# PEER grids: a turn after each of the first four one-hot steps of a tile

## The chip, the cores and the metric

The kernel runs on one core of one Trainium2 chip. The metric is the device time of one execution in microseconds, here the median of several executions. One execution was also taken by the hardware profiler; its trace is what the rows below come from.

## What is computed

The reference runs three transformer layers on 512 tokens of width 1024, in float32: a layer with an RWKV-7 time mix and a SwiGLU, a layer with a spatial gating unit and a SwiGLU, and a layer with two kinds of attention and a PEER feed-forward. The change lies in the PEER part alone, which the reference writes so:

```
q = (hb @ w_q).reshape(C, PEER_HEADS, 2, PEER_DK_HALF)
s = einsum('thpd,hpnd->thpn', q, sub_keys)
sv, si = lax.top_k(s, PEER_TOPK)
cand = sv[:, :, 0, :, None] + sv[:, :, 1, None, :]
cidx = si[:, :, 0, :, None] * PEER_NKEYS + si[:, :, 1, None, :]
fv, fpos = lax.top_k(cand, PEER_TOPK)
eidx = take_along_axis(cidx, fpos)          # 8 heads x 16 = 128 experts of 16384 for each token
g = softmax(fv)
a = gelu(einsum('ted,td->te', u_tab[eidx], hb))
return einsum('te,ted->td', g * a, v_tab[eidx])
```

## The kernel before

The tokens are four tiles of 128. The kernel treats tile 0 and tiles 1 to 3 of the PEER part in two different ways.

**Tiles 1 to 3, dense.** The 16384 experts are 128 groups of 128. `act(j)` loads group j of the u table (512 KB, `wload`, queue SP), splits it into a high part `whi` (ScalarE) and a low part `wlo` (VectorE; for every fifth group GpSimd), multiplies both with the 384 tokens in 24 matmuls (L122 to L124, `mm3`) and puts the gelu into `gl` (L1274). The generator `ahead` runs `act` for the first 112 groups ahead of their use and stores each `gl` to DRAM as `ga[j]` (L1279, queue of GpSimd); `fill(n)` takes n of these steps. The last 16 groups are made inside the last loop (`late_act`, tile `gla`). Below, "an act" is one such step.

**The grids.** How much weight a token gives to each expert is built as a 128 x 128 grid for each token: the product of a one-hot matrix of the expert's first index (scaled by the softmax weight in two float16 parts, `oi`) and one of its second index (`oj`). `onehots(t)` makes both for four tokens at a time, one set, in four steps on VectorE: `on` (L1451, copied to `oj` by ScalarE, L1452), `os` (L1454), and `oi` twice (L1457). There are two buffers for `on` and `os` and three for `oi` and `oj`. `grids(t)` first runs four such steps (HL = 4, so one set ahead). Then, 32 times for a tile, it runs four more steps, multiplies the oldest set in eight matmuls (L1477) and copies the bank into `G` (ScalarE, L1479). `G` goes to DRAM in pieces of 512 KB (`spill`, tile `gd`, queue SP), but for the last two of twelve, which stay on chip.

**Tile 0, gathered.** `own` fetches the 128 chosen u rows and then the 128 chosen v rows of tile 0's tokens by indirect DMA (L1297, 512 KB each, up to five ahead) and does one VectorE pass over each (L1309 with an accumulator read for u, L1313 for v): 256 steps. `some(x)` adds x to a debt and takes a step for each whole one.

**How the work is interleaved.** `picks(t)` finds the top experts of a tile on VectorE (L1342 to L1436) and gives a turn back 14 times. At each turn the driver at the end of `peer` lets `unit(prev, 3)` take three turns of the grids of the tile before. Each turn that `grids` gives back also pays for other work: FG = 0.6508 acts (FL = 0.7484 in tile 3) and S2 = 0.7 steps of `own` (SL = 0.8 in tile 3). After the last tile, `fill(NS)` takes the acts that are left, and the last loop over all 128 groups begins: it loads `ga[j]` back into `gl` (L1571, queue SP), multiplies it with the grid table `gte` or `gtl` (L1573, read from `gd` by L1549 in pieces of 640 KB for four groups, queue of GpSimd) and with the `G` on chip (L1575), splits it (`ch`, `cl`), loads a group of the v table and does 18 matmuls. Each round pays for S3 = 1.2492 steps of `own`.

The Python order is not the order on the engines: a scheduler places the instructions on each engine's queue when the program is built, and the engines run these queues in order.

The four lines that the change stands in:

```
hot = onehots(t, hots)
for _ in range(HL):
    next(hot)
for c in range(128 // CT):
```

Of the kernel before, what the change touches and what calls it, by code (L numbers as in the profile page):

```python
# [40 lines left out]
class Kern:  # L41
# [1198 lines left out]
    def peer(self):  # L1240
# [8 lines left out]
        with ExitStack() as cx:  # L1249
# [192 lines left out]
            def onehots(t, done):  # L1442
                sh = [128, OT // 4, 128, 4]
                of = lambda v: v.rearrange("p (g t) -> p g t", t=4)[:, :, None, :].to_broadcast(sh)
                io = io4[:, None].to_broadcast(sh)
                for tk in range(t * 128 - 128, t * 128, OT):
                    os, on = [q4.tile(sh, F16, name=n) for n in ("os", "on")]
                    oi = q4.tile([128, 2] + sh[1:], F16, name="oi", bufs=OB)
                    oj = q4.tile([128, OT, 128], F16, name="oj", bufs=OB)
                    done.append((oi, oj))  # L1450
                    nc.vector.tensor_tensor(on, io, of(JT[:, tk:tk + OT]), op=OP.is_equal)  # L1451
                    nc.scalar.copy(oj, on.rearrange("p g i t -> p (g t) i"))  # L1452
                    yield
                    nc.vector.tensor_tensor(os, io, of(IT[:, tk:tk + OT]), op=OP.is_equal)  # L1454
                    yield
                    for w in range(2):
                        nc.vector.tensor_mul(oi[:, w], os, of(WW[:, w, tk:tk + OT]))  # L1457
                        yield

            def grids(t):  # L1460

                gout = iter(())
                hots = []
                hot = onehots(t, hots)
                for _ in range(HL):
                    next(hot)
                for c in range(128 // CT):
                    G = gp.tile([128, 128, CT], F32, name="G")
                    for u in range(0, CT, 4):
                        bk = self.bank("x")  # L1470
                        for _ in range(16 // OT):
                            next(hot, None)
                        if u % OT == 0:
                            oi, oj = hots.pop(0)
                        for e in range(4):
                            for w in range(2):
                                mm(bk[:, e * 128:(e + 1) * 128], oi[:, w, u % OT // 4, :, e], oj[:, u % OT + e],  # L1477
                                   start=(w == 0), stop=(w == 1))
                        nc.scalar.activation(G[:, :, u:u + 4], bk.rearrange("p (t j) -> p j t", t=4), AF.Copy,  # L1479
                                             scale=1.0 / WSC)  # L1480
                        if u % 8 == 4:
                            next(gout, None)
                        yield
                    n = (t - 1) * (128 // CT) + c
                    gout = spill(n, G)
                    if n >= CD - KG:
                        last.append(G)
                        gout = iter(())
                for _ in gout:
                    pass  # L1490

            def spill(c, G):
                for k in range(0, 128, 2048 // CT // 2):
                    n = 2048 // CT // 2
                    nc.sync.dma_start(gd[c, 0:128, k * CT:(k + n) * CT], G[:, k:k + n].rearrange("p j t -> p (j t)"))
                    yield
# [19 lines left out]
            for t in range(NT):  # L1516
                if t == 0:
                    for _ in picks(t):
                        pace(FA, 0)
                    for u in range(1, NT):  # L1520
                        for _ in tops(u):
                            pace(FT, S0)
                    cs.close()
                    q4 = cy.enter_context(tc.tile_pool(name="pe3b", bufs=2))
                    gp = cx.enter_context(tc.tile_pool(name="pegg", bufs=2, side="right"))
                    prev = iter(())
                    continue
                for _ in picks(t):
                    pace(FB, S1)
                    unit(prev, 3)  # L1530
                unit(prev, 128)
                late[0] = t - 1
                prev = grids(t)
# [155 lines left out]
```

## Time and profile before

| | |
|---|---|
| median of 3 executions | 3034.14 us (3032.5 to 3037.2) |
| the profiled execution | 3031.09 us |
| its span in the trace | 3029.4 us |
| TensorE (PE) busy | 2900.9 us, 96% |
| VectorE (DVE) busy | 2090.2 us, 69% |
| ScalarE (ACT) busy | 1208.0 us, 40% |
| GpSimd (POOL) busy | 641.1 us, 21% |

The profile's shares are averages over the whole span; the PEER part, from about 1710 us on, has several stretches with different limits, so it is read by stretches. In the trace the first one-hot row of tile 1 starts at 1993.6 us, that of tile 2 at 2121.2 us and that of tile 3 at 2243.5 us; the last grid matmul ends at 2354.3 us, the last act of the tail at 2391.9 us. A matmul's end is modelled and overlaps the next one's start, so for TensorE the time of a step is taken from counts and stretches rather than from the mean of one row.

### The profile page before, as it was taken

The numbers are of one execution on the slowest core, as the hardware profiler recorded it, in microseconds if no ns is written. First come the engines' busy times: TensorE is split into PE (matmuls) and PEld (weight loads), VectorE is DVE, ScalarE is ACT, GpSimd is POOL, SyncE is SP. The second block draws the span as 40 slices with busy tenths as digits, with TensorE's granted clock in tenths as the row PEclk, the third lists the DMA queues.
The fourth block names the chain that finished last, engine by engine and source line by source line (L and its number), as shares of the span: only waits on it lengthen the run. The fifth ranks groups of instructions, "written<-read, shape, count | busy, mean of one in ns | idle before, by whom it ended". The sixth has DMA issues, their size and how long they took to land.

```text
span 3029.4 us, 43851 instructions
## 1 busy us (share of the span) xinstructions
PE 2900.9 (96%) x16121; PEld 2438.7 (81%) x16121; DVE 2090.2 (69%) x4710; ACT 1208.0 (40%) x2014; POOL 641.1 (21%) x577
## 2 busy tenths in 40 slices
PE   7988989999999999999999999989999999999998
PEld 6867877888888788888875888888999888878787
DVE  6774776333255766425776678999998478878787
ACT  5544333322223422223565433355655333333332
POOL 1022220000000000000000003335455344444443
PEclk9989999999999999999988999999999999999999
DMA  4357553323333277432220234679889899999896
GB/s 142 98 145 213 142 143 115 102 93 95 93 132 103 79 246 237 135 91 90 84 72 8 70 96 165 226 244 320 292 326 322 298 319 345 327 330 318 304 328 225
DMA packets 218579, 569.05 MB, mean 188 GB/s; under 512 B 64474, under 2 KB 80090, under 8 KB 218236
## 3 DMA queue, kind: packets, MB, share of 16 engines
q1 hardware_dynamic: 144508, 362.71, 36.7%
q0 software_dynamic: 62816, 196.70, 19.0%
q10 hardware_dynamic: 11040, 6.84, 0.8%
q8 instruction: 127, 2.08, 0.3%
q14 instruction: 88, 0.72, 0.1%
HBM read 504.24 MB, written 61.87 MB: 187 GB/s over the span
## 4 chain that ended last, share of the span: by engine, by line
PE 66%; DVE 17%; DMA 9%; issue 4%; ACT 3%; POOL 1%; DVEq 0%; POOLq 0%; ACTq 0%; SPq 0%
PE b L276 20%; PE b L124 12%; PE b L123 12%; PE b L122 12%; DMA gl<-ga 4%; DVE wlo L103 3%; DVE er L1309 2%; DVE oi L1457 1%; DVE hr L1313 1%; PE b L1166 1%; DMA wst<-in_pe_v 1%; PE b L1477 1%; PE b L964 1%; PE b L1184 1%; DVE cl L103 1%
## 5 line engine op out<-in xcount | busy, mean ns | idle before, releaser
L102 ACT CAST whi<-wst 128x1024 fp32r<-128x1024 f32 (+2 forms) x491 | 510.6, 1042 | 1067.2 <-PE b L123 334.6
L103 DVE TENSOR_TENSOR wlo<-wst,whi 128x1024 fp32r<-128x1024 f32 (+2 forms) x466 | 563.4, 1210 | 425.2 <-ACT whi L102 408.5
L124 PE MATMUL b<-hTh,wlo 128*128 128x384 f32 (+2 forms) x1992 | 716.5, 360 | 15.1 <-DVE wlo L103 14.9
L122 PE MATMUL b<-hTh,whi 128*128 128x384 f32 (+2 forms) x1992 | 722.5, 363 | 2.5 <-ACT hTh L223 1.5
L123 PE MATMUL b<-hTl,whi 128*128 128x384 f32 (+2 forms) x1992 | 717.2, 360 | 2.2 <-DVE hTl L224 2.2
L124 PEld LDWEIGHTS b<-hTh,wlo 128*128 128x128 f32 x1992 | 378.5, 190 | 58.6 <-DVE wlo L103 21.1
L122 PEld LDWEIGHTS b<-hTh,whi 128*128 128x128 f32 x1992 | 379.0, 191 | 42.0 <-ACT hTh L223 2.2
L123 PEld LDWEIGHTS b<-hTl,whi 128*128 128x128 f32 x1992 | 379.1, 190 | 40.8 <-DVE hTl L224 3.0
L123 PE MATMUL b<-wlo,ch 128*128 128x512 f32 x768 | 306.6, 399 | 6.2 <-DVE wlo L103 6.1
L122 PE MATMUL b<-whi,ch 128*128 128x512 f32 x768 | 306.3, 399 | 5.2 <-ACT ch L102 5.2
L124 PE MATMUL b<-whi,cl 128*128 128x512 f32 x768 | 306.3, 399 | 1.3 <-DVE cl L103 1.3
L1297 POOL DMA_INDIRECT er<-in_pe_v,ev x128 | 196.0, 1531 | 248.0 <-DVE hr L1313 222.3
L1297 POOL DMA_INDIRECT er<-in_pe_ur,eu x128 | 174.0, 1360 | 88.6 <-DVE er L1309 57.7
L123 PEld LDWEIGHTS b<-wlo,ch 128*128 128x128 f32 x768 | 145.8, 190 | 42.2 <-DVE wlo L103 8.0
L122 PEld LDWEIGHTS b<-whi,ch 128*128 128x128 f32 x768 | 145.8, 190 | 39.9 <-ACT ch L102 5.5
L124 PEld LDWEIGHTS b<-whi,cl 128*128 128x128 f32 x768 | 145.8, 190 | 36.7 <-DVE cl L103 2.0
L1309 DVE SCALAR_TENSOR_TENSOR er<-er,hr 128x1024 f32<-128x1024 f32 x128 | 161.9, 1269 | 10.1 <-DMA er<-in_pe_ur,eu 10.1
L1313 DVE SCALAR_TENSOR_TENSOR hr<-er,a,hr 128x1024 f32<-128x1024 f32 x127 | 166.8, 1313 | 0.1
L1279 POOL DMA_DIRECT2D ga<-gl x112 | 64.9, 579 | 318.7 <-ACT gl L1274 307.5
L276 PE MATMUL b<-whi,hTh 128*128 128x512 f32 (+2 forms) x336 | 129.4, 387 | 0.8 <-ACT P L976 0.8
L276 PE MATMUL b<-whi,hTl 128*128 128x512 f32 (+2 forms) x336 | 129.5, 386 | 0.4 <-DVE hTl L103 0.4
L276 PE MATMUL b<-wlo,hTh 128*128 128x512 f32 (+2 forms) x336 | 129.7, 386 | 0.0
(557 smaller groups left out, 4911.8 us busy)
## 6 DMA issues: line engine op xcount, KB each, us to landing
wst<-in_pe_u SPq DMA_DIRECT2D x128, 512.0 KB, 5.4
wst<-in_pe_v SPq DMA_DIRECT2D x128, 512.0 KB, 6.1
wst<-in_ffn_gu SPq DMA_DIRECT2D x88, 512.0 KB, 3.3
wst<-in_ad_w SPq DMA_DIRECT2D x48, 512.0 KB, 3.9
wst<-in_ffn_dn SPq DMA_DIRECT2D x44, 512.0 KB, 3.6
ga<-gl POOLq DMA_DIRECT2D x112, 192.0 KB, 4.9
gl<-ga SPq DMA_DIRECT2D x112, 192.0 KB, 5.3
gd<-G SPq DMA_DIRECT2D x40, 512.0 KB, 8.1
```

Of the source, the lines that this page charges most:

```text
L102: self.nc.scalar.copy(hi, src)
L103: (eng or self.nc.vector).tensor_sub(lo, src, hi)
L122: mm(out, a[0], b[0], start=start, stop=False)
L123: mm(out, a[0], b[1], start=False, stop=False)
L124: mm(out, a[1], b[0], start=False, stop=stop)
L276: self.nc.tensor.matmul(banks[t][:, :n], self.chunk(aT, a, k + kk)[:, t * 128:(t + 1) * 128], w[b][:, kk, :], start=seen[t] == 1, stop=see ...
L964: self.nc.tensor.transpose(bk[:, c * 128:(c + 1) * 128], src[:, c * 128:(c + 1) * 128], self.ident)
L1166: mm(ob[:, h * 128:(h + 1) * 128], PT[:, k, :], v[k][:, h, :], start=(k == 0), stop=(k == t))
L1279: nc.gpsimd.dma_start(ga[j], act(j))
L1297: d = nc.gpsimd.indirect_dma_start(out=r, out_offset=None, in_=src, in_offset=bass.IndirectOffsetOnAxis(ap=idx[:, k:k + 1], axis=0))
L1309: d = nc.vector.scalar_tensor_tensor(r, r, 1.0, hr, op0=OP.mult, op1=OP.mult, accum_out=a0[:, k:k + 1])
L1313: d = nc.vector.scalar_tensor_tensor(y0, r, a0[:, k - 128:k - 127], y0, op0=OP.mult, op1=OP.add)
```

## The change

`grids` now gives a turn back after each of the first four one-hot steps of a tile:

```diff
@@ -1464,6 +1464,7 @@
                 hot = onehots(t, hots)
                 for _ in range(HL):
                     next(hot)
+                    yield
                 for c in range(128 // CT):
```

So a tile's grids give 36 turns instead of 32, and the driver pays for acts and steps of `own` at 108 turns instead of 96. No constant is changed: 72 turns at 0.6508 and 36 at 0.7484 make 73.8 acts where it were 65.6, and 72 at 0.7 and 36 at 0.8 make 79.2 steps of `own` where it were 70.4. With the 39 acts that other places take, all 112 are taken before `fill(NS)`, where eight were left for it. No instruction is added or removed on any engine; they stand in another order. Lines behind the change carry a number that is higher by one.

**VectorE, the beginning of tile 1's grids** (`wlo` belongs to an act, `er` to a step of `own`; `on`, `os` and two `oi` are one set of four tokens). Before:

```order
L103 TENSOR_TENSOR wlo<-wst,whi 128x1024
L1451 TENSOR_TENSOR on<-io_14630,JT 128x512
L1454 TENSOR_TENSOR os<-io_14630,IT 128x512
L1451 TENSOR_TENSOR on<-io_14630,JT 128x512
L1457 TENSOR_TENSOR oi<-os,WW 128x512 x2
L1454 TENSOR_TENSOR os<-io_14630,IT 128x512
L1451 TENSOR_TENSOR on<-io_14630,JT 128x512
L1457 TENSOR_TENSOR oi<-os,WW 128x512 x2
L1309 SCALAR_TENSOR_TENSOR er,a_14638<-er,hr 128x1024
```

Now:

```order
L103 TENSOR_TENSOR wlo<-wst,whi 128x1024
L1451 TENSOR_TENSOR on<-io_14630,JT 128x512
L1309 SCALAR_TENSOR_TENSOR er,a_14638<-er,hr 128x1024
L1454 TENSOR_TENSOR os<-io_14630,IT 128x512
L1309 SCALAR_TENSOR_TENSOR er,a_14638<-er,hr 128x1024
L1457 TENSOR_TENSOR oi<-os,WW 128x512
L1309 SCALAR_TENSOR_TENSOR er,a_14638<-er,hr 128x1024
L1457 TENSOR_TENSOR oi<-os,WW 128x512
L1451 TENSOR_TENSOR on<-io_14630,JT 128x512
L1454 TENSOR_TENSOR os<-io_14630,IT 128x512
L103 TENSOR_TENSOR wlo<-wst,whi 128x1024
L1457 TENSOR_TENSOR oi<-os,WW 128x512 x2
```

Steps of `own` and a split stand between the first set's four steps. On TensorE three acts, 72 matmuls, now stand ahead of the first grid matmul of each tile; before, the first grid matmuls of tiles 1 and 2 stood inside an act.

**GpSimd's queue at the end of tile 3's grids** (`ga` is the store of an act, and its number counts up to 14616 for the last one; `gte` and `gtl` are the grid tables of the last loop). Before:

```order
L1279 DMA ga_14605<-gl 128x384
L1549 DMA gte<-gd 128x10x128 x2
L103 TENSOR_TENSOR wlo<-wst,whi 128x1024
L1279 DMA ga_14606<-gl 128x384
L1297 DMA er<-in_pe_ur,eu 128x1024
L1549 DMA gtl<-gd 128x10x128
L1279 DMA ga_14607<-gl 128x384
L1297 DMA er<-in_pe_ur,eu 128x1024 x2
L1549 DMA gte<-gd 128x10x128
```

Now:

```order
L1279 DMA ga_14613<-gl 128x384
L1297 DMA er<-in_pe_ur,eu 128x1024
L1550 DMA gte<-gd 128x10x128 x2
L1279 DMA ga_14614<-gl 128x384
L1297 DMA er<-in_pe_ur,eu 128x1024
L1550 DMA gtl<-gd 128x10x128
L1279 DMA ga_14615<-gl 128x384
L1297 DMA er<-in_pe_ur,eu 128x1024
L1550 DMA gte<-gd 128x10x128
L1550 DMA gtl<-gd 128x10x128
L1279 DMA ga_14616<-gl 128x384
```

The first table load stood eleven acts before the last one and stands three before it now. On ScalarE's queue nine acts' gelu stood behind the last copy of a grid bank; now none does, and the first `ch` of the last loop follows it at once.

## Rows read from the trace of the kernel before

**Rows 1.** The page: busy time, share of the span and instructions of each engine.

```profile
PE 2900.9 (96%) x16121; PEld 2438.7 (81%) x16121; DVE 2090.2 (69%) x4710; ACT 1208.0 (40%) x2014; POOL 641.1 (21%) x577
```

**Rows 2.** Windows: tiles 1, 2, 3, tail, switch, a piece of the last loop.

```profile
core 0: us, PE busy (x) PEld busy (x) DVE busy (x) ACT busy (x) POOL busy (x), PEclk, DMA share, GB/s
1993.60:2121.20 127.60, 118.11 (x811) 112.83 (x811) 125.54 (x271) 72.58 (x117) 62.08 (x51) 0.95 0.81 286
2121.20:2243.50 122.30, 118.60 (x828) 113.83 (x829) 121.45 (x247) 75.58 (x121) 62.22 (x54) 0.97 0.85 303
2243.50:2354.30 110.80, 110.21 (x797) 106.46 (x796) 96.34 (x185) 64.97 (x107) 63.84 (x53) 1.00 0.91 323
2354.30:2391.90 37.60, 37.60 (x218) 37.28 (x216) 12.09 (x12) 13.13 (x21) 15.78 (x19) 1.00 0.90 319
2391.90:2400.20 8.30, 1.82 (x4) 1.01 (x5) 5.29 (x14) 2.32 (x4) 1.98 (x3) 0.62 0.98 348
...
2700.00:2900.00 200.00, 192.92 (x841) 158.26 (x840) 156.85 (x255) 66.11 (x90) 86.84 (x60) 0.98 0.91 315
```

**Rows 3.** Timeline of TensorE at the first grid matmuls of tiles 1 and 2.

```profile
1988.00 0.33 PE L124 MATMUL b<-hTh,wlo 128*128 128x384 f32 x1
1995.18 0.27 PE L1477 MATMUL b<-oj,oi 128*128 128x128 f16 x1 [6.84 <-DVE oi L1457]
...
2115.97 0.34 PE L124 MATMUL b<-hTh,wlo 128*128 128x384 f32 x1
2122.68 0.29 PE L1477 MATMUL b<-oj,oi 128*128 128x128 f16 x1 [6.38 <-DVE oi L1457]
```

**Rows 4.** Groups of VectorE in tiles 1 and 2: count | busy, mean ns | idle.

```profile
L1309 DVE SCALAR_TENSOR_TENSOR er<-er,hr 128x1024 f32<-128x1024 f32 x52 | 67.8, 1305 | 0.0
L1457 DVE TENSOR_TENSOR oi<-os,WW 128x512 f16<-128x512 f16 x134 | 54.4, 452 | 0.1
L103 DVE TENSOR_TENSOR wlo<-wst,whi 128x1024 fp32r<-128x1024 f32 x38 | 46.4, 1220 | 0.2 <-ACT whi L102 0.2
L1454 DVE TENSOR_TENSOR os<-io,IT 128x512 f16<-128x512 f16 x68 | 34.7, 517 | 0.0
L1451 DVE TENSOR_TENSOR on<-io,JT 128x512 f16<-128x512 f16 x64 | 32.1, 502 | 2.5 <-ACT oj L1452 2.3
...
L1309 DVE DVE_READ_ACCUMULATOR er<-er,hr 128x1 f32 x52 | 4.4, 84 | 0.0
```

**Rows 5.** Timeline: a split on GpSimd and the VectorE row beside it.

```profile
2095.27 2.79 POOL L103 TENSOR_TENSOR wlo<-wst,whi 128x1024 fp32r<-128x1024 f32 x1 [0.49 <-ACT whi L102]
2095.69 3.45 DVE L1309 SCALAR_TENSOR_TENSOR er<-er,hr 128x1024 f32<-128x1024 f32 x1
```

**Rows 6.** Groups of TensorE in the tail, 2354.3 to 2391.9 us.

```profile
L122 PE MATMUL b<-hTh,whi 128*128 128x384 f32 x72 | 24.2, 337 | 0.0
```

**Rows 7.** Timelines of TensorE, SP and VectorE at the switch to the last loop.

```profile
2390.50 3.36 SPq L1571 DMA_DIRECT2D gl<-ga  x3
...
2391.57 0.33 PE L124 MATMUL b<-hTh,wlo 128*128 128x384 f32 x1
...
2395.82 0.49 DVE L1573 TENSOR_TENSOR gl<-gl,gte 128x320 f32<-128x320 f32 x1 [0.61 <-DMA gl<-ga]
...
2397.11 0.80 PE L122 MATMUL b<-whi,ch 128*128 128x512 f32 x1 [5.21 <-ACT ch L102]
```

**Rows 8.** DMA issues, 2354 to 2400 us: count, size, median us to landing.

```profile
gtl<-gd POOLq DMA_DIRECT2D x2, 640.0 KB, 11.1
gl<-ga SPq DMA_DIRECT2D x5, 192.0 KB, 5.1
```

**Rows 9.** DMA issues in tile 3, 2243 to 2354 us.

```profile
gd<-G SPq DMA_DIRECT2D x8, 512.0 KB, 8.4
```

**Rows 10.** The chain that ended last: a long load in the last loop.

```profile
2701.38 10.12 DMA gl<-ga
```

## The prediction

> **What bounds the kernel now.** I read the page first, for which engine could be the limit at all; then a table of windows cut at the stages of the PEER part, for which engine is full in which stage; then the timeline at the places where TensorE stands, for what it waits for; last the groups of rows and the DMA table, for prices. The page says that TensorE is busy 96% of the span [rows 1]. The matmuls themselves are not changed, so a reordering can win only what TensorE stands, or give it more to stand.
>
> The windows tell where that is [rows 2]. In tiles 1 and 2 VectorE is full: 125.54 of 127.60 us and 121.45 of 122.30 us, while TensorE is busy 118.11 and 118.60 us. It stands 9.5 and 3.7 us there, and a granted clock of 0.95 and 0.97 says that a part of the rest ran at the lower of the two levels, 1.2 GHz. In tile 3 it is the other way round: TensorE has 110.21 of 110.80 us, VectorE 96.34. The tail, the acts that were left over for after the grids, is TensorE alone: 37.60 of 37.60 us, with VectorE at 12.09. Then comes the switch to the last loop: 8.3 us in which TensorE is busy 1.82 us. In the last loop it stands little, 7.1 us in the worst 200 us.
>
> So work of TensorE is done in a stretch that TensorE bounds (the tail) while it stands in two stretches that VectorE bounds. The two longest stops are at the first grid matmul of tile 1, after 6.84 us, and of tile 2, after 6.38 us, both ended by `oi` [rows 3].
>
> **The change, part by part.**
>
> *What moves.* Twelve turns more. Those of tiles 1 and 2 pay for 8 x 0.6508 = 5.2 acts and 8 x 0.7 = 5.6 steps of `own`; those of tile 3 for 4 x 0.7484 = 3.0 acts and 4 x 0.8 = 3.2 steps. I count in VectorE's order from the first one-hot row of tile 1 to that of tile 3: `own` 52 before and 58 now, splits 37 and 42, `oi` 134 and 130, everything that belongs to `picks` 84 and 84.
>
> *A. VectorE in tiles 1 and 2: +12.6 us.* It is full there, so what it gets more is time. Six steps of `own` at 1.305 + 0.084 us are 8.3 us, five splits at 1.220 us 6.1 us, four `oi` fewer at 0.452 us take 1.8 us off [rows 4]. Bounds: VectorE had 2.06 + 0.85 = 2.9 us free in these two windows [rows 2], so +9.7 at the least. One in five acts is split on GpSimd, and then a VectorE row beside it can take 3.45 instead of 1.305 us [rows 5]; two such collisions more would make it +17. I take the sum as it stands, since the means of rows 4 already hold the collisions at the present rate.
>
> *B. TensorE from tile 3 on: -21.7 us.* From there to the end of the tail it is the bound, so this stretch lasts as long as the acts that are left. 72 x 3 matmuls make the tail of 37.6 us, nine acts of 24 matmuls [rows 2, 6]: 4.18 us an act. With 5.2 acts more done in tiles 1 and 2, 5.2 x 4.18 = 21.7 us fewer are left. Bound on the other side: five splits on VectorE go with one on GpSimd, so it may be six acts, -25.1 us. The room is there: A lengthens tiles 1 and 2 by 12.6 us, so TensorE must use 21.7 - 12.6 = 9.1 of the 13.2 us that it stands in them, and what it lost at the lower clock besides.
>
> *C. Tile 3's own four turns and the tail: 0.* They move three acts from the tail into tile 3. Both are bound by TensorE, so an act costs 4.18 us on either side. VectorE gets 3.2 x 1.389 + 3 x 1.220 = 8.1 us more in tile 3, where 110.80 - 96.34 = 14.5 us are free [rows 2, 4]; that cover holds.
>
> *D. The switch: +3 us.* Before, `gl` is asked for at 2390.50 us, the tail's last matmul starts at 2391.57 us, `gl` is multiplied at 2395.82 us and the last loop starts at 2397.11 us [rows 7]. This load stands behind weight loads whose buffers come free with the splits of the last acts, now as before, so the chain keeps its length. But nine acts lay between the last grid matmul and this place, and they covered the grid tables. The first table load stood eleven acts before the last and stands three before it now. Five of 640 KB are 3.28 MB; at the 348 GB/s that the switch reached [rows 2] they are 9.4 us of transfer. Three acts with the grid matmuls between them are about 14 us. In these, tile 3 has spare 348 - 323 = 25 GB/s, 0.35 MB, and the spills, 8 x 0.512 MB in 110.8 us or 37 GB/s [rows 9], have ended by then, another 0.5 MB. So 2.4 MB or 7 us are pushed into the switch, and only the first table of five, one `gl` and one group of v are needed to start: I take less than half, +3. Bounds: -1, if all is there in time and the last grid step covers a piece of the chain, and +9.4, if everything must land first.
>
> A load of `gl` landed in 5.1 us in the stretch in which a table took 11.1 [rows 8]. The Trainium skill, "DMA: Bandwidth & Descriptors", section "Queues, rings and completion order", says that a transfer's signal lands only after every earlier write of the same DMA engine, across its queues. By that rule `gl`, asked for behind the tables, would be held until they have landed; D would be +9.4 and the sum that of rival 1. The rows don't decide it, since those loads of `gl` began after the tables had landed.
>
> *E. The last loop: -1 us.* Nine steps of `own` leave it: 9 x 0.524 MB are 4.7 MB or 15 us of transfer at 315 GB/s [rows 2]. TensorE bounds this loop, though, and stands 7.1 us in its worst 200 us, where loads of `gl` take up to 10.12 us instead of a median of 5.1 [rows 8, 10]. So the gain lies between 0 and 7; as these stops are few, I take 1. Two more queues are passed over at nothing: SP issues the same loads in nearly the same order, and ScalarE is busy 64.97 us of tile 3's 110.80 [rows 2], so three acts more fit.
>
> *The sum.* +12.6 - 21.7 + 0 + 3 - 1 = -7.1 us against the profiled execution's 3031.09 us: 3024.0 us. The median of the runs shown, 3034.14 us, lies 3.05 us above that execution, so I say 3027 us for the median. A change of 0.2%, 6.1 us, is about what a measurement of this kernel tells from none.
>
> **The rivals.**
>
> *1. The switch takes it all: no change.* The nine acts were the cover of the tables, and all five must land before the last loop gets going. For it speaks that the tables took 11.1 us each even beside the tail [rows 8] and that tile 3's transfers are at a share of 0.91 already [rows 2]; against it, that only the first of them is needed. With D at its bound of +9.4 and E at 0 the sum is 12.6 - 21.7 + 9.4 = +0.3: 3034 us. The page's rule under D speaks for it too. Chance 0.28.
>
> *2. VectorE waits for TensorE at each tile's fourth set: slower.* There are three buffers for `oi`, so the fourth set's first `oi` waits for the first grid matmuls, and these stand behind three acts now. TensorE can be there 1.2 + 3 x 4.18 + 0.5 = 14.2 us after the first split starts. (The 0.5 us are one grid step: of tile 3's 797 matmuls 256 are grid matmuls, and 110.21 us less 541 x 0.174 us leave 0.063 us for each, eight of them 0.5 us [rows 2].) VectorE's rows to that place are three splits, four steps of `own`, four `on`, four `os` and six `oi`: 3.7 + 5.6 + 4.1 + 2.7 = 16.1 us [rows 4]. So by the sum there is no wait, with 1.9 us to spare. It decides as soon as the three acts come later than that, say because a group of u lands late. If they are two acts, 8.4 us, late at both tiles, VectorE loses 6.5 us each time where it is the bound, 13 us in all: 3027 + 13 = 3040 us. For it speaks that TensorE stands at just this place now [rows 3] and that it is the one place where the new order makes VectorE depend on acts; against it, that all three splits stand on VectorE's queue and GpSimd's ahead of the fourth set. Chance 0.17.
>
> *3. VectorE's part is free too: much faster.* If VectorE's free 2.9 us are used up, A is at its lower bound, and if six acts come in and the switch covers itself, the sum is 9.7 - 25.1 - 1 - 3 = -19 us, 3015 us. Against it speaks that VectorE's rows show no idle time worth the name in tiles 1 and 2 [rows 4]. It is counted within "faster".
>
> **How the numbers follow.** The forecast, with rival 3 as its far end, has 0.55; of this 0.05 ends within 0.2% by the spread of D alone. Faster by over 0.2%: 0.50. Within 0.2%: 0.28 + 0.05 = 0.33. Slower by over 0.2%: rival 2 with 0.17. That the change does nothing is excluded, since the order shows the acts moved. The range takes in rival 3 at its low end and reaches to just under rival 2's price at the high end, where half of rival 2 is left out: 3015 to 3040 us.
>
> **What would show it.** Tail and switch: no stretch of TensorE alone without VectorE between the last grid matmul and the last loop. A: the first one-hot row of tile 3 comes some 12 us later than at 2243.5 us, and VectorE is still full until then. B: the last act ends about 9 us before 2391.9 us. D: the stop of TensorE before the first matmul with `ch` is 5 to 9 us, ended by `ch` behind a load of `gl` or a table; over 15 us means rival 1. Rival 2 would show as `oi` waiting for L1477 for several us near the beginning of each tile. The forecast is wrong if tile 3 begins over 22 us later, for then the acts moved bought nothing.

## The result, and the profile after

The changed kernel is slower: 3050.52 us (median of 15 runs, 3037.3 to 3068.67) against 3031.89 us (15 runs, 3022.26 to 3044.18), a ratio of 1.0059 with a 95% interval of 1.0042 to 1.0076. The profiled execution took 3050.3 us with a span of 3048.3 us, so it is a typical one. The prediction had said 3027.0 us and gave 0.17 to "slower".

The page of the changed kernel, its line of busy time:

```profile
PE 2904.2 (95%) x16121; PEld 2436.8 (80%) x16121; DVE 2088.9 (69%) x4710; ACT 1209.6 (40%) x2014; POOL 639.5 (21%) x577
```

TensorE has the same 16121 matmuls and is busy 3.3 us more than in [rows 1]; the other 15.6 us of the longer span are standing. Where, the windows of the same stages tell: tiles 1, 2 and 3 with the end of the grids, the switch, two pieces of the last loop.

```profile
core 0: us, PE busy (x) PEld busy (x) DVE busy (x) ACT busy (x) POOL busy (x), PEclk, DMA share, GB/s
1990.70:2128.60 137.90, 129.13 (x880) 124.01 (x881) 136.58 (x303) 79.65 (x126) 69.02 (x57) 0.98 0.82 294
2128.60:2265.20 136.60, 129.98 (x888) 124.51 (x886) 118.46 (x226) 76.34 (x123) 71.61 (x61) 0.99 0.85 308
2265.20:2387.30 122.10, 121.94 (x854) 118.11 (x854) 105.18 (x201) 71.10 (x116) 74.17 (x63) 0.99 0.88 312
2387.30:2405.40 18.10, 2.01 (x7) 1.08 (x5) 6.45 (x16) 2.48 (x6) 7.54 (x8) 0.64 1.03 368
2405.40:2700.00 294.60, 285.82 (x1235) 234.54 (x1234) 226.20 (x401) 98.30 (x135) 116.39 (x87) 0.98 0.90 314
```

Against [rows 2] the stages add up to the whole difference of the two spans, 3048.3 - 3029.4 = 18.9 us:

| stretch | before | after | change | forecast |
| --- | --- | --- | --- | --- |
| up to tile 1's grids (nothing is moved there) | 1993.6 | 1990.7 | -2.9 | 0 |
| tiles 1 and 2 | 249.9 | 274.5 | +24.6 | +12.6 (A) |
| tile 3 and tail | 148.4 | 122.1 | -26.3 | -21.7 (B, C) |
| switch | 8.3 | 18.1 | +9.8 | +3 (D) |
| last loop to the end | 629.2 | 642.9 | +13.7 | -1 (E) |

The tail is gone as forecast, and tiles and tail together gain 1.7 us. Switch and last loop lose 23.5. Three views show by what. First VectorE's waits in tiles 1 and 2:

```profile
engine line waited for: us in total, times, longest us
DVE er L1309 <- DMA er<-in_pe_ur,eu: 13.6, 3, 8.3
```

Before, VectorE had no such wait in these two tiles (in tile 3 it had four, 6.4 us together); a step of `own` now reaches the head of its queue before its gathered row has landed. All three of these waits lie in tile 2, where VectorE is busy 118.46 of 136.60 us; in tile 1 it is still full, 136.58 of 137.90. Over both it was busy 125.54 + 121.45 = 246.99 of 249.9 us, and is now busy 255.04 of 274.5 us.

TensorE at the first grid matmul of tile 1, where [rows 3] showed stops of 6.84 and 6.38 us:

```profile
1994.74 0.25 PE L1478 MATMUL b<-oj,oi 128*128 128x128 f16 x1
1995.60 0.58 PE L1478 MATMUL b<-oj,oi 128*128 128x128 f16 x7 [0.61 <-DVE oi L1457]
```

These two stops are gone; in tile 2 no grid matmul near the beginning waits for `oi` either. The switch, VectorE first, then TensorE, to be read beside [rows 7]:

```profile
2391.96 1.22 DVE L1309 SCALAR_TENSOR_TENSOR er<-er,hr 128x1024 f32<-128x1024 f32 x1 [6.78 <-DMA er<-in_pe_ur,eu]
...
2398.10 1.22 DVE L1309 SCALAR_TENSOR_TENSOR er<-er,hr 128x1024 f32<-128x1024 f32 x1 [3.77 <-DMA er<-in_pe_ur,eu]
2399.25 0.08 DVE L1309 DVE_READ_ACCUMULATOR er<-er,hr 128x1 f32 x1
2399.25 0.49 DVE L1574 TENSOR_TENSOR gl<-gl,gte 128x320 f32<-128x320 f32 x1
```

```profile
2400.54 0.80 PE L122 MATMUL b<-whi,ch 128*128 128x512 f32 x1 [13.12 <-ACT ch L102]
...
2404.73 0.79 PE L124 MATMUL b<-whi,cl 128*128 128x512 f32 x1 [2.97 <-DVE cl L103]
```

The first product of `gl` stands on VectorE behind two steps of `own` that wait 6.78 and 3.77 us for their rows. The DMA issues of 2360 to 2410 us, beside [rows 8]:

```profile
gl<-ga SPq DMA_DIRECT2D x7, 192.0 KB, 8.0
gtl<-gd POOLq DMA_DIRECT2D x2, 640.0 KB, 14.8
er<-in_pe_ur,eu POOLq DMA_INDIRECT x13, 11.9
```

And TensorE's waits in the last loop, 2405 to 3015 us, after and then before:

```profile
PE b L123 <- DVE wlo L103: 11.1, 7, 2.7
PE b L124 <- DVE wlo L103: 5.6, 3, 2.7
```

```profile
PE b L123 <- DVE wlo L103: 6.1, 2, 4.3
PE b L124 <- DVE wlo L103: 2.1, 3, 0.9
```

TensorE stands there twice as long, 16.7 us instead of 8.2, each time for the second half of a split of weights: in the seven stops of L123 for weights v, in the three of L124 for those of an act made inside the loop. These stops come at one place of the loop: in rounds 12, 20, 36, 44, 60, 68, 76, 92 and 100, all of the form 8k + 4. So 8.5 of the 13.7 us are these stops; besides, TensorE is busy 5.4 us longer for the same 2696 matmuls from the first `ch` on (618.73 instead of 613.38 us), at a granted clock of 0.98 instead of 0.99. The change moves nothing inside this loop but the account of `own` (the debt that `some` keeps), which comes out of the grids at 1.0 instead of 0.2. With 1.2492 steps a round, the rounds that hold two steps are then 0, 4, 8 ... instead of 3, 7, 11 ... .

### The profile page after: what moved, and what is told of

It is laid out like the page before. It is cut to its first block, busy times and chain, and to the rows that moved or that the text cites. A ratio compares the mean times of both kernels' runs of the same rounds, so it can differ in the third digit from the quotient of the medians.

```text
span 3048.3 us, 43840 instructions
## 1 busy us (share of the span) xinstructions
PE 2904.2 (95%) x16121; PEld 2436.8 (80%) x16121; DVE 2088.9 (69%) x4710; ACT 1209.6 (40%) x2014; POOL 639.5 (21%) x577
## 3 DMA queue, kind: packets, MB, share of 16 engines
q10 hardware_dynamic: 11040, 6.84, 0.8%
## 4 chain that ended last, share of the span: by engine, by line
PE 61%; DVE 18%; DMA 11%; issue 5%; ACT 2%; POOL 2%; SPq 0%; POOLq 0%; DVEq 0%; ACTq 0%
PE b L276 19%; PE b L124 11%; PE b L123 11%; PE b L122 11%; DMA gl<-ga 6%; DVE wlo L103 3%; DVE er L1309 2%; DVE hr L1313 1%; DMA er<-in_pe_ur,eu 1%; DMA wst<-in_pe_v 1%; DVE oi L1457 1%; PE b L1166 1%; DVE cl L103 1%; POOL er L1297 1%; PE b L964 1%
## 5 line engine op out<-in xcount | busy, mean ns | idle before, releaser
L124 PE MATMUL b<-hTh,wlo 128*128 128x384 f32 (+2 forms) x1992 | 720.4, 362 | 26.7 <-DVE wlo L103 25.8
L123 PE MATMUL b<-hTl,whi 128*128 128x384 f32 (+2 forms) x1992 | 719.7, 362 | 3.1 <-DVE hTl L224 3.1
L124 PEld LDWEIGHTS b<-hTh,wlo 128*128 128x128 f32 x1992 | 380.9, 191 | 74.1 <-DVE wlo L103 35.1
L123 PEld LDWEIGHTS b<-hTl,whi 128*128 128x128 f32 x1992 | 381.2, 191 | 41.7 <-DVE hTl L224 3.7
L122 PE MATMUL b<-whi,ch 128*128 128x512 f32 x768 | 306.0, 398 | 13.1 <-ACT ch L102 13.1
L123 PE MATMUL b<-wlo,ch 128*128 128x512 f32 x768 | 306.8, 400 | 11.1 <-DVE wlo L103 11.1
L124 PE MATMUL b<-whi,cl 128*128 128x512 f32 x768 | 306.2, 399 | 3.0 <-DVE cl L103 3.0
L1297 POOL DMA_INDIRECT er<-in_pe_v,ev x128 | 189.4, 1480 | 259.6 <-DVE hr L1313 246.7
L123 PEld LDWEIGHTS b<-wlo,ch 128*128 128x128 f32 x768 | 145.7, 190 | 49.0 <-DVE wlo L103 14.8
L124 PEld LDWEIGHTS b<-whi,cl 128*128 128x128 f32 x768 | 145.6, 190 | 38.3 <-DVE cl L103 3.7
```

The costliest lines, as they stand in the source:

```text
L122: mm(out, a[0], b[0], start=start, stop=False)
L123: mm(out, a[0], b[1], start=False, stop=False)
L124: mm(out, a[1], b[0], start=False, stop=stop)
L1297: d = nc.gpsimd.indirect_dma_start(out=r, out_offset=None, in_=src, in_offset=bass.IndirectOffsetOnAxis(ap=idx[:, k:k + 1], axis=0))
```

## The experiments

A number in brackets is the ratio to the kernel before, run on the same chip, with its 95% interval. Its median in these runs was 3028.0 to 3032.9 us.

**First: is it the acts, the steps of `own`, or the place of the turn?** My theory was that the steps of `own` cost, by their gathers in the tiles and by the account that they leave; the rivals were the cover that went with the tail, and the turn's place as such. In these four kernels the turn stays. With all four constants lowered, the grids pay for as much as before:

```diff
-FA, FT, FB, FG, FL = .2, .5, .2, .6508, .7484
-S0, S1, S2, SL, S3 = .3, .2, .7, .8, 1.2492
+FA, FT, FB, FG, FL = .2, .5, .2, .6508 * 8 / 9, .7484 * 8 / 9
+S0, S1, S2, SL, S3 = .3, .2, .7 * 8 / 9, .8 * 8 / 9, 1.2492
```

> The change with its four prices of a turn in the grids (FG, FL, S2, SL) times 8/9, so that 36 turns pay for what 32 paid for: 104 acts and 93 steps of own before the last loop, as before; the turns stay. Theory A (the counts do it: acts and own steps pulled ahead of the switch): as the kernel before, within 5 us, a tail of nine acts, a switch of 8 us. Theory B (the turn itself does it: three acts ahead of a tile's first grid matmul): still 10 to 20 us slower than before, with tiles 1 and 2 longer.

Measured: 3046.53 us, 1.0060 (1.0043 to 1.0078). Its profiled run was its fastest, 3036.35 us; tile 2 took 139.1 us there, switch and last loop were as before. I ran it again below.

Only the first of the two lines (acts as before, with their tail; `own` as after):

> The change with FG and FL alone times 8/9: 104 acts as before, so the tail of nine acts is back, but own as in the change. Cover theory (the tail hid the grid tables): switch back to 8 us from 18. Phase theory (own's two-step rounds fall on rounds 0, 4, 8 of the last loop instead of 3, 7, 11, which puts two gl loads ahead of a v load on SP): last loop still some 14 us longer than before. Both true: 10 us faster than the change and 8 to 14 us slower than before.

Measured: 3050.93 us, 1.0075 (1.0049 to 1.0102). Giving the tail back takes nothing off the loss.

Only the second line (`own` as before; all acts in the grids, no tail):

> The change with S2 and SL alone times 8/9: own as before (93 steps ahead of the last loop, two-step rounds 3, 7, 11), all acts in the grids, no tail. Phase theory: last loop as before, 14 us shorter than in the change. Cover theory: the switch stays at 15 us or more. Both true: 12 to 14 us faster than the change, 0 to 10 us slower than before. If the gathers and not the missing tail make the switch long, it falls to 10 us and the time to that of before or under it.

Measured: 3032.57 us, 1.0010 (0.9995 to 1.0024). Among the changed kernel and these two, the loss goes with the steps of `own`, not with the acts and the cover they gave (the first kernel, which has neither and still loses, doesn't fit; see below). These steps carry two things: they are done earlier, and they leave another account for the last loop. The fourth kernel separates the two, with all counts of the changed kernel:

```diff
             fill(NS)
+            due[0] -= .8
```

> The change with 0.8 taken from own's debt ahead of the last loop: two-step rounds 3, 7, 11 as in the kernel before, everything before the loop as in the change. Phase theory: 10 to 14 us faster than the change, all of it in the last loop; switch still 18 us. If the phase does nothing (the loop is late because it starts with nothing fetched ahead): no difference to the change beyond 4 us.

Measured: 3035.93 us, 1.0016 (0.9996 to 1.0036), 14.6 us less than the changed kernel. In its profile, though, the last loop was hardly shorter: 646.1 us from the first `ch` on against 647.8. Counted from the first `cl`, behind the switch's two stops, it took 637.7 against 643.6, and 629.8 in the kernel before. So the account's part still had to be shown by itself.

**Second: the account alone, without any turn.**

```diff
             fill(NS)
+            due[0] += .8
```

> The kernel before, without any new turn, with 0.8 added to own's account after the last act, so that the rounds of the last loop with two steps of own are 0, 4, 8 ... instead of 3, 7, 11 ...; nothing ahead of the last loop differs. SP then issues two loads of gl ahead of a load of v once in eight rounds, as in the changed kernel. Theory P (the phase of own in the last loop costs, by itself): 3030 + 10 to 15 = 3040 to 3045 us, the last loop 643 to 647 us instead of 632.3, with a stop at one round in eight, ended by wlo. Theory Q (the phase costs only together with the full transfers that the missing tail leaves behind, or the difference of the two earlier kernels was chance): 3027 to 3033 us, the last loop 630 to 635 us.

Measured: 3043.55 us, 1.0054 (1.0034 to 1.0075). Its last loop, from the first `ch` on, takes 642.4 us instead of 632.3, tiles 1 and 2 take 253.5 instead of 249.9. One number that shifts which rounds of the last loop hold two steps of `own` costs 12.6 us, two thirds of the change's loss.

The kernel before, again without the turn, with the same four constants raised by 9/8:

> The kernel before, without the new turn, but with the four constants of the grids' turns raised by 9/8, so that its 96 turns pay for as many acts and steps of own as the 108 turns of the changed kernel: 28 or 29 steps and 22 splits in a tile, one act left behind the grids, two-step rounds 0, 4, 8 ... in the last loop. Theory C (the counts and the phase do it, the place of the four turns nothing): as the changed kernel, 3046 to 3053 us. Theory T (the place does it: acts and steps between the first one-hot steps): only the phase's price or nothing, 3030 to 3042 us, and tiles 1 and 2 together 260 to 266 us instead of 274.5.

Measured: 3054.95 us, 1.0089 (1.0058 to 1.0120); tiles 1 and 2 took 275.6 us, against 274.5 with the turn. The counts do this as well as the turn does; the place of the turn is not needed for it.

The first experiment once more:

> The turn with all four constants lowered by 8/9, once more, for a second profile and twice the runs: as many acts and steps of own as before, the tail and the two-step rounds of before. Theory T (the place of the turns costs by itself, in tile 2 above all): again 3043 to 3050 us, with tiles 1 and 2 together 262 to 270 us. Theory N (the first result was the spread of few runs): 3028 to 3036 us. If the profile falls on a typical run near 3046 us, its last loop tells where the rest sits: 630 to 634 us puts it all in the tiles, 640 us and more in the loop.

Measured: 3039.87 us, 1.0031 (1.0013 to 1.0049), less than the first time but still a loss, with tile 2 at 138.2 us again and tile 3 at 105.0 us instead of 110.8. So the turn in its place, with counts and account as before, costs something too. The largest waits of TensorE and of VectorE in tiles 1 and 2:

```profile
PE b L1478 <- ACT oj L1452: 12.6, 5, 3.5
```

```profile
DVE er L1309 <- DMA er<-in_pe_ur,eu: 11.7, 5, 4.9
```

VectorE stands for gathered rows as in the changed kernel, though no step of `own` was added. Why this form, which does fewer acts in the tiles, loses in tile 2 what the form with all acts (third kernel above, with 1.5 us of these waits) does not, I didn't separate.

**Third: by what way does the account cost?** SP's order differs with it: once in eight rounds two loads of `gl` stand ahead of a load of v. I pinned these loads to the order of the program, in the kernel with the shift:

```diff
-                    nc.sync.dma_start(gl, ga[j])
+                    tc.keep_in_program_order(nc.sync.dma_start(gl, ga[j]))
...
-        self.nc.sync.dma_start(v(st), src)
+        d = self.nc.sync.dma_start(v(st), src)
+        if pin:
+            self.tc.keep_in_program_order(d)
```

> The kernel before with only the shift of own's two-step rounds to 0, 4, 8 ... (as the run that shifted the phase alone, 3043.6 us), and SP's loads of the last loop pinned to the order of the program: one load of gl, one of v, in turn, and nowhere two loads of gl ahead of one of v. Theory S (the shift costs by way of SP's order: a load of v behind two of gl): 3026 to 3034 us, the stops ended by wlo once in eight rounds gone. Theory V (it costs by VectorE's own order, two steps of own ahead of a split, whatever SP does): 3040 to 3047 us with the same stops.

Measured: 3051.48 us, 1.0072 (1.0046 to 1.0097). Theory S falls; theory V's range was passed too. The same pin in the changed kernel:

> The changed kernel with SP's loads of the last loop pinned to the order of the program, nothing else. Theory S: it loses the phase's price, 12 to 15 us: 3034 to 3040 us, as the changed kernel with the phase of before had (3035.9). Theory V: as the changed kernel, 3047 to 3054 us. Below 3028 us it would beat both kernels.

Measured: 3056.75 us, 1.0089 (1.0058 to 1.0121), no gain. In the kernel before:

> The kernel before with SP's loads of the last loop pinned to the order of the program, own's rounds as before. It tells what the pin costs or gives by itself. Theory S: the two pairs of gl in eight rounds that the order of before still has cost little or nothing, so 3024 to 3032 us; if the pin holds loads back (a load of gl comes one or two rounds later than in the order of before), 3034 to 3042 us, and the other two pinned runs must be read against it.

Measured: 3028.7 us, 1.0004 (0.9984 to 1.0024): SP's order costs nothing that shows here. And another shift, by 0.25:

> The kernel before with 0.25 added to own's account after the last act: two-step rounds 2, 6, 10 ... . SP's order is then that of the shifted kernel (two loads of gl ahead of a load of v once in eight rounds), but the round with two steps of own is another one. Theory S (SP's order decides): 3039 to 3046 us as for rounds 0, 4, 8. Theory V (the place of own's two-step round decides): it may be anything from 3026 to 3046 us, and 3026 to 3034 us would speak against S.

Measured: 3066.87 us, 1.0132 (1.0103 to 1.0162), far above theory S's range. TensorE's waits in its last loop:

```profile
PE b L123 <- DVE wlo L103: 23.4, 16, 3.7
PE b L124 <- DVE wlo L103: 11.0, 7, 2.8
```

So the place of the two-step rounds decides, and SP's order doesn't explain it; VectorE's order was the next suspect. One of TensorE's stops, in the kernel with the shift of 0.8, VectorE's rows and then ScalarE's and TensorE's:

```profile
2574.53 0.49 DVE L1574 TENSOR_TENSOR gl<-gl,gte 128x320 f32<-128x320 f32 x1
2574.94 0.29 DVE L1576 TENSOR_TENSOR gl<-gl,G 128x32 f32<-128x32 f32 x2
2578.74 0.49 DVE L1574 TENSOR_TENSOR gl<-gl,gte 128x320 f32<-128x320 f32 x1 [3.52 <-DMA gl<-ga]
2579.15 0.56 DVE L103 TENSOR_TENSOR cl<-gl,ch 128x384 fp32r<-128x384 f32 x1
2579.62 0.29 DVE L1576 TENSOR_TENSOR gl<-gl,G 128x32 f32<-128x32 f32 x2
2579.82 1.22 DVE L103 TENSOR_TENSOR wlo<-wst,whi 128x1024 fp32r<-128x1024 f32 x1
```

```profile
2573.84 1.05 ACT L102 CAST whi<-wst 128x1024 fp32r<-128x1024 f32 x1 [1.35 <-DMA wst<-in_pe_u]
2581.63 1.05 ACT L102 CAST whi<-wst 128x1024 fp32r<-128x1024 f32 x1 [6.74 <-DMA wst<-in_pe_v]
```

```profile
2581.10 0.50 PE L123 MATMUL b<-wlo,ch 128*128 128x512 f32 x1 [3.17 <-DVE wlo L103]
```

No `whi` is made between 2574.9 and 2581.6 us, so the `whi` that this `wlo` needs was there at 2574.9 us at the latest. VectorE could have split then; instead it stood 3.52 us at the head of its queue for a load of `gl` that a later round needs. I followed every stop of TensorE over 0.3 us behind a `wlo` of VectorE back in this way: in 9 of 9 in this kernel, and in 9 of 10 in the changed one, one of the six rows ahead of the split is a product that waited for its `gl`. That place alone makes no stop, though: of the 138 splits of weights that VectorE makes in this loop, 42 stand so, and in the kernel before 57 of 138, most of them without a stop. What the shift changes is when they come, and these rows don't show why.

Two edits tell whether it is the ring of `gl`'s buffers or the place of the split. The first gives `gl` a fifth buffer:

```diff
-ERB, LAG, CB, GB, PG, GP, AL = 6, 5, 5, 3, 4, 1, 2
+ERB, LAG, CB, GB, PG, GP, AL = 6, 5, 5, 3, 5, 1, 2
```

> The kernel before with own's two-step rounds shifted to 0, 4, 8 ... (3043.6 us with four buffers for gl) and a fifth buffer for gl. In the trace of the shifted kernel SP stands in front of a load of gl until VectorE's cl frees a buffer, VectorE stands 3.5 us in front of a product for an earlier load of gl, and the load of v behind them is issued 7.7 us after the one before it. Theory K (this ring of buffer, product and load is how the shift costs): 3027 to 3035 us, stops of the last loop as before. Theory L (it is the split's own place behind two steps of own on VectorE, whatever the buffers): 3040 to 3047 us.

Measured: 3040.62 us, 1.0040 (1.0017 to 1.0063); theory K falls.

> The changed kernel with a fifth buffer for gl. Theory K: 3030 to 3039 us, the last loop 632 to 637 us instead of 647.7. Theory L: 3046 to 3054 us.

Measured: 3048.12 us, 1.0046 (1.0019 to 1.0073): no gain that shows.

> The kernel before with a fifth buffer for gl and nothing else, which tells what the buffer gives by itself. Theory K: 3020 to 3030 us, since the ring closes a few times in the kernel before too. Theory L: 3027 to 3033 us.

Measured: 3019.67 us, 0.9965 (0.9940 to 0.9989), faster than both kernels. The buffer helps the order of before and hardly the shifted one.

> The kernel before with 0.5 added to own's account after the last act: two-step rounds 1, 5, 9 ..., the fourth and last place that they can have. Rounds 3, 7, 11 took 3030 us, 0, 4, 8 took 3043.6 and 2, 6, 10 took 3066.9. If the rounds before had been a lucky place (the constants stood at the best of four): 3040 to 3070 us. If only even rounds are bad, since the late act stands at a round of the form 8k + 4 to 8k + 7: 3026 to 3036 us.

Measured: 3041.34 us, 1.0037 (1.0015 to 1.0059). With it all four places have been timed: rounds 3, 7, 11 about 3030 us, 1, 5, 9 3041, 0, 4, 8 3044, 2, 6, 10 3067. The kernel before stood at the best of them, and nearly any edit that changes the steps of `own` leaves it.

The second edit puts each round's weights ahead of its products of `gl` in the program, so that VectorE's queue has the split first:

```diff
+                v = self.wload(I["pe_v"][j], [128, 1024])
                 g8 = gl.rearrange("p (c t) -> p c t", c=CD)
...
                 self.split(ch, cl, gl)
-                v = self.wload(I["pe_v"][j], [128, 1024])
                 some(S3)
```

In the kernel with the shift of 0.8:

> The kernel before with own's two-step rounds shifted to 0, 4, 8 ... (3043.6 us), and each round's weights loaded and split ahead of its products of gl in the program, so that VectorE's queue has the split of v ahead of products that wait for loads of gl. In the trace of the shifted kernel each stop of TensorE in the last loop is ended by a wlo whose whi was ready 3 to 6 us before, and which stood on VectorE behind such a product. Theory M (the place of the split behind a product that waits for its load is how the shift costs): 3026 to 3035 us, PE's waits for wlo in the last loop at most 6 us. Theory O (the place of the split is a symptom, transfers are late anyway): 3039 to 3048 us.

Measured: 3016.21 us, 0.9958 (0.9939 to 0.9977). The shift's price is gone, with more on top, and below theory M's range; TensorE's waits in its last loop:

```profile
PE b L123 <- DVE wlo L103: 2.8, 2, 2.3
PE b L124 <- DVE wlo L103: 0.4, 1, 0.4
```

In the changed kernel:

> The changed kernel with each round's weights loaded and split ahead of its products of gl. Theory M: 3031 to 3039 us, the last loop 632 to 638 us instead of 647.7, and the rest of the loss, 2 to 7 us, in the tiles and the switch. Theory O: 3046 to 3054 us.

Measured: 3030.97 us, 1.0011 (0.9994 to 1.0028), 19.6 us less than the changed kernel as it is. Its profiled run was its fastest, 3021.81 us. It is 14.8 us above the shifted kernel with the same edit, so with this cost taken away the change still loses; with the account put back the rest was 4 to 7 us (fourth kernel). Between these two numbers the runs leave it open.

In the kernel before with the fifth buffer:

> The kernel before with the fifth buffer for gl (3019.7 us) and the splits ahead of the products; without the turn. It is meant to beat both kernels. Theory M: 3012 to 3020 us. Theory O: 3017 to 3025 us, as with the buffer alone.

Measured: 3009.3 us, 0.9935 (0.9909 to 0.9961), the fastest of all, without the turn: 41 us below the changed kernel. The kernel before with this edit alone wasn't run. Beside the fifth buffer, without any shift, the edit gave 10.4 us (3019.67 to 3009.3); so of the 27.3 us that it gave the shifted kernel some 10 are likely a gain of its own, and the rest, some 17, covers the shift's 12.6.

## Why the prediction was wrong, point by point

*What moves* held: 58 steps of `own`, 42 to 43 splits on VectorE and 130 `oi` stand in tiles 1 and 2, and the tail is gone.

*A, +12.6 us* was mis-sized: +24.6. The step that failed is "it is full there, so what it gets more is time". The added work is there, VectorE is busy 255.04 - 246.99 = 8.05 us more, but it now also stands 19.5 us instead of 2.9, 13.6 of them for the gathers of `own`, whose rows landed in a median of 8.0 and 8.2 us in tiles 1 and 2 instead of 6.8 and 6.6. I priced a step of `own` by its busy time and not by the landing of its row. That is not the whole of it: with `own` as before and 1.5 us of these waits (third kernel) tiles 1 and 2 still took 265.9 us, 16.0 more than before, where A has 6.1 - 1.8 = 4.3 us for the acts alone. Which term takes how much isn't shown.

*B, -21.7 us* held in its mechanism and was somewhat low (-26.3 with C). But *the room is there* failed: TensorE should have used 9.1 of the 13.2 us that it stood in tiles 1 and 2; it stands 8.77 + 6.62 = 15.4 us there now. Its busy time there rose from 236.71 to 259.11 us, 22.4 us, so the moved acts lengthened these tiles by about what they took off the tail. Its two long stops went, and shorter ones came in their place, for `wlo` 7.2 us instead of 2.0. *C, 0*, is contained in this sum and not seen by itself; VectorE's cover in tile 3 held, 105.18 of 122.10 us.

*D, +3 us* was mis-sized: +9.8, its upper bound. "Only the first table of five, one `gl` and one group of v are needed to start" overlooked the acts' own stores, and so did "this load stands behind weight loads". `gl` has four buffers, which the acts and the last loop share, so a load of `gl` waits for the store that still reads its buffer. SP's waits from 2354 to 2400 us in the kernel before showed it already:

```profile
SPq L1571 <- DMA ga<-gl: 6.4, 2, 4.5
```

The chain of waits through the switch has, before and after:

```profile
2389.34 4.06 DMA ga<-gl
2393.54 4.93 DMA gl<-ga
```

```profile
2383.89 12.53 DMA ga<-gl
2396.50 7.12 DMA gl<-ga
```

The store of the act before the last one landed in 12.53 instead of 4.06 us beside the tables, and the third load of `gl` started only behind it and took 7.12 instead of 4.93: 10.7 us more, about D. Giving `own` back doesn't cure it, although two of its steps stand ahead of the first product: the kernels without a tail that have `own` or its account as before stood 9.7 + 6.3 and 9.2 + 7.2 us for the first `ch` and `cl`, as much as the 13.1 + 3.0 here. Nor is the store's chain all of it: with a fifth buffer for `gl` the changed kernel still stood 11.4 + 0.5 us, against 5.6 in the kernel before with that buffer. The rule of the Trainium skill cited under D (page "DMA: Bandwidth & Descriptors", section "Queues, rings and completion order") would have given the +9.4. The trace agrees with it in size (+9.8) alone; since the store goes through the same queue as the tables, it doesn't show whether a transfer of another queue is held too.

*E, -1 us* had the wrong sign: +13.7. The step that failed is "nine steps of `own` leave it", which counted the steps and not the account they leave, and "SP issues the same loads in nearly the same order", which looked at the wrong queue. By the constants it is eight steps (101 instead of 93 are taken before the loop, the account holds the ninth), and they leave only the loop's end, since each round pays as before: the last step of `own` starts 38.6 us before the span's end instead of 17.4. The account moves the two-step rounds, VectorE's order moves with them, and splits of weights that stand behind a product waiting for `gl` come too late for TensorE. The shift alone cost 12.6 us, and putting the splits first gave 27 back, some 10 of them likely a gain of its own. That all of E in the changed kernel is the account isn't shown: with the account put back (fourth kernel) the profiled loop got back 5.9 of its 13.8 us, counted from the first `cl`.

*The rivals.* Rival 1 had the switch's price right (+9.4) and the rest not, so its 3034 us failed as well. Rival 2 did not happen: TensorE's waits for `oi` in tiles 1 and 2 fell from 16.2 to 5.9 us, and VectorE waits for no grid matmul there. The kernel ended slower, but by none of its mechanism. Rival 3 failed with A. Of the signs named, tile 3 began 21.7 us later by the trace's clock and 24.6 us later counted from tile 1's start, about at the 22 us from which the forecast was to be wrong; the last act ended 4.5 us earlier, not 9.

## What to carry to other kernels

Work that is paid out by an account has a phase: when an edit changes how much is paid in one stage, compute where the account leaves the next one, and compare the order of the engine that serves both there, even if nothing in that stage was edited. On an engine with one queue in order, put what the bound engine needs next (here the split of the weights) ahead of what may wait for a transfer; here that gave more than the balancing between stages. Price a moved step by when its data lands as well as by its busy time. And time that an engine stands in a stage isn't yet room for moved work: here TensorE stood 13.2 us in two tiles, was given 22.4 us more to do, and stood 15.4 us.

## What the runs showed of the hardware that was not expected

A store of 192 KB landed in 12.53 us instead of 4.06 while tables of 640 KB were in flight at a DMA share of 1.03. One and the same kernel spreads over 22 us (3022.26 to 3044.18 in the first comparison), and a single profile may fall on its fastest run, as it did four times here with kernels whose medians lay 9 to 17 us higher; a stage of a few us is read from it, a verdict is not.
